# The last matrix of an expert layer multiplied over picked experts only, on one Trainium2 core

## The chip, the core and the metric

The kernel runs on one core of a Trainium2 chip, in one launch. The metric is the device time of that launch in microseconds (us). TensorE's matmuls are called PE, its weight loads PEld, VectorE DVE, ScalarE ACT, GpSimd POOL; SP is the queue that issues most of the loads.

## What is computed

Two transformer blocks on 256 tokens of width 2048, in float32. The second one ends in a layer of 16384 experts, 128 x 128 pairs of keys: each token picks 16 experts in each of 8 heads, and only the picked ones count for it.

```python
def block(xt):                                   # 128 tokens at a time
    q = (xt @ wq).reshape(-1, PEER_HEADS, 2, PEER_HALF)
    s = jnp.einsum('thpc,hpnc->thpn', q, keys)
    sv, si = lax.top_k(s, PEER_TOPK)
    ...
    top_s, top_j = lax.top_k(cand, PEER_TOPK)
    eid = jnp.take_along_axis(cid, top_j, axis=-1)
    gate = jax.nn.softmax(top_s.astype(jnp.float32), axis=-1)
    ue = jnp.take(u, eid, axis=0)
    act = jax.nn.gelu(jnp.einsum('thkd,td->thk', ue, xt).astype(jnp.float32), approximate=False)
    ve = jnp.take(v, eid, axis=0)
    return jnp.einsum('thk,thkd->td', (gate * act).astype(xt.dtype), ve)
...
h = layernorm(ALPHA * h + ff, ln2_g[l], ln2_b[l])
```

## The kernel before

All weights come as chunks of 128 x 1024 in the order of their use, through `Stream`: SP loads a chunk into `raw`, ACT copies it to `whi` (its upper bits, line 116), DVE subtracts to get `wlo` (line 99), some chunks ahead of PE. A product of float32 matrices is three matmuls of such parts: `colmm` (lines 265 to 267) with the weights standing, `tokmm` (lines 272 to 274) with the tokens standing. `Fill` holds side work as generators; `tick()` between chunks lets each go one step further, so the written order of the ticks sets where the side work stands in each engine's queue. No scheduler moves anything.

The last two stages take all experts, dense. In the u stage a tile `i1` is one first key with its 128 second keys, two chunks, 48 matmuls of 256 columns; there are 128 tiles and two ticks in each. The gelu of a tile goes into the activations, tiles of 128 experts x 256 tokens held in three buffers, `fx` (0 to 31), `act0` (32 to 55) and `act1` (56 to 127). From tile N0 = 56 on the side work is `weigh`: by groups of four tokens it makes one-hot vectors of each token's 128 pairs of keys (`eq` and `o2` by DVE, line 1195, two tokens an instruction; three products on POOL with the gates, lines 1198 and 1200), multiplies them on PE (line 1223, eight small matmuls a group) and so gets the sums of the gates of all pairs of keys. Tiles that are there are multiplied by them on DVE (line 1214), for the others they are copied into the place by ACT (line 1216) and the tile's gelu is multiplied later (line 1246). A group takes two ticks.

In the v stage the columns are done in two halves, 128 chunks each: `split` makes two parts of a tile's activations (ACT line 1260, DVE line 1261), and each chunk is multiplied with both halves of the tokens into four accumulators, 12 matmuls of 512 columns. The residual and the last norm's rows are loaded by POOL in between (lines 1292 and 1294). At the end come the last norm's statistics (`evac3`, `stats3`) and `apply3` by blocks of 512 columns on DVE (lines 1327, 1328) or ACT and POOL (lines 1323 to 1325), and the stores.

Of the kernel before, what the change touches and what calls it, by code (L numbers as in the profile page):

```python
# [13 lines left out]
U32 = mybir.dt.uint32  # L14
AF = mybir.ActivationFunctionType
# [5 lines left out]
D = 2048  # L21
KT = 16
T = 256
# [12 lines left out]
AHEAD = 3  # L36
GSCALE = 1024.0

# column table: per-feature parameters, one column of 128 features each
# [3 lines left out]
# row table: parameters broadcast over the partitions  # L43
# [3 lines left out]
class Stream:  # L47
    """Weight chunks [128, 1024] in the order of their use: loaded ahead, and split into two
    parts of 12 significant bits each that add up to the value. The first `n0` chunks have
    buffers of their own, those in `whole` stay as they are, and those in `extra` are split into  # L50
    the slots of `slots`, so that more of them than usual can be held."""
# [14 lines left out]
    def part(self, c, x):  # L66
        """a buffer for the first or the second part of chunk c, if there is one"""
# [76 lines left out]
class Fill:  # L144
    """Work that runs between the chunks of the products, on two lanes."""
# [35 lines left out]
def block(ctx, tc, a):  # L181
# [4 lines left out]
    # the weight chunks in the order of their use  # L186
# [40 lines left out]
    ch += [a["v"][i] for i in range(256)]  # L227
# [17 lines left out]
    # those of no use to the last stage  # L245
# [16 lines left out]
    def colmm(ps, w, wl, xh, xl, first, last, own=True):  # L262
        """ps += w' x in three products of parts"""
# [5 lines left out]
    def tokmm(ps, xh, xl, w, wl, first, last, own=True):  # L269
        """ps += x' w in three products of parts"""  # L270
# [5 lines left out]
    # ------------------------------------------------------------------ modulation  # L276
# [36 lines left out]
    # silu(c), silu(c_ctx) in two parts  # L313
# [19 lines left out]
    def stats_x(l):  # L333
# [14 lines left out]
        # var ** -1/2, and a Newton step  # L348
# [84 lines left out]
    def rope_gen(tile_):  # L433
        """axial rope in place on tile_[:, 0:2, :T]"""
# [98 lines left out]
    def gate_evac(ps, half, g):  # L533
        """mixed = silu(gate) * attention, in two parts"""
# [19 lines left out]
    def in_block(kind, half, g, ps):  # L554
        """a block of 256 columns, chunk by chunk"""
# [85 lines left out]
    # lam  # L641
# [27 lines left out]
    # ------------------------------------------------------------------ first output, norms  # L669
# [101 lines left out]
    def apply(tt):  # L771
        """the normed tokens in place, with the mean in mv and the scale in sm[3]"""
# [9 lines left out]
    def stats1(tt):  # L782
        # the first norm's scale r and the second's are one: r (r^2 var + e)^-1/2 = (var + e / r^2)^-1/2
# [399 lines left out]
    def weigh(l):  # L1183
# [6 lines left out]
        def onehots(n):  # L1190
            if n >= T // 2:
                return
# [251 lines left out]
```

## Time and profile before

| | |
|---|---|
| median of 3 runs | 2898.07 us (2896.87 to 2898.65) |
| span of the profiled execution | 2896.3 us |
| PE busy in the span | 2836.4 us, 18864 matmuls |
| DVE, ACT, POOL busy | 1920.3, 1270.1, 489.3 us |
| moved by DMA | 522.44 MB |

The profile is of one execution. The u stage runs from 1382 us (its first loads) to 2179 us, the v stage from there to the end. Matmuls are pipelined, so the duration of a single one is longer than the time from one to the next; the latter is what counts.

### The profile page before, as it was taken

The numbers are of one execution on the slowest core, as the hardware profiler recorded it, in microseconds if no ns is written. First come the engines' busy times: TensorE is split into PE (matmuls) and PEld (weight loads), VectorE is DVE, ScalarE is ACT, GpSimd is POOL, SyncE is SP. The second block draws the span as 40 slices with busy tenths as digits, with TensorE's granted clock in tenths as the row PEclk, the third lists the DMA queues.
The fourth block names the chain that finished last, engine by engine and source line by source line (L and its number), as shares of the span: only waits on it lengthen the run. The fifth ranks groups of instructions, "written<-read, shape, count | busy, mean of one in ns | idle before, by whom it ended". The sixth has DMA issues, their size and how long they took to land.

```text
span 2896.3 us, 47924 instructions
## 1 busy us (share of the span) xinstructions
PE 2836.4 (98%) x18864; PEld 2536.3 (88%) x18864; DVE 1920.3 (66%) x3028; ACT 1270.1 (44%) x1865; POOL 489.3 (17%) x564
## 2 busy tenths in 40 slices
PE   6999999999989999999999999999999999999997
PEld 1588889889879999989999999999998888888885
DVE  7766556444566665564888879999965656666566
ACT  6533334224454444454444444444445545455453
POOL 2000010000120000001000018888830000000001
PEclk8999999999999999999999999999999999999998
DMA  9734345444645555656666555555557666676664
GB/s 335 282 114 132 126 125 186 148 133 130 215 155 186 175 161 176 196 181 197 204 182 182 183 176 167 162 167 163 165 174 220 194 191 196 197 218 195 191 195 138
DMA packets 143650, 522.44 MB, mean 180 GB/s; under 512 B 16496, under 2 KB 16768, under 8 KB 143168
## 3 DMA queue, kind: packets, MB, share of 16 engines
q1 hardware_dynamic: 133648, 484.40, 53.4%
q0 software_dynamic: 9344, 34.32, 3.7%
q8 instruction: 148, 2.42, 0.3%
q14 instruction: 78, 0.64, 0.1%
q10 hardware_dynamic: 432, 0.66, 0.1%
HBM read 515.12 MB, written 4.19 MB: 179 GB/s over the span
## 4 chain that ended last, share of the span: by engine, by line
PE 92%; DVE 3%; DMA 2%; ACT 1%; issue 1%; POOL 0%; SPq 0%; DVEq 0%; ACTq 0%; POOLq 0%
PE acc L265 16%; PE acc L267 16%; PE acc L266 16%; PE acc L273 8%; PE acc L272 8%; PE acc L274 8%; PE lane L273 4%; PE lane L274 4%; PE lane L272 4%; PE acc L372 2%; PE lane L1223 1%; DMA raw<-in_w_out 1%; DVE wlo L99 1%; PE lane L452 1%; PE lane L478 0%
## 5 line engine op out<-in xcount | busy, mean ns | idle before, releaser
L99 DVE TENSOR_TENSOR wlo<-raw,whi 128x1024 fp32r<-128x1024 f32 x881 | 1116.1, 1270 | 620.1 <-issue 167.0
L116 ACT CAST whi<-raw 128x1024 fp32r<-128x1024 f32 x881 | 922.8, 1050 | 1074.5 <-PE acc L266 399.7
L265 PE MATMUL acc<-ga,whi 128*128 128x256 f32 x3024 | 862.3, 285 | 0.0
L267 PE MATMUL acc<-ga,wlo 128*128 128x256 f32 x3024 | 855.4, 283 | 0.4 <-DVE wlo L99 0.4
L266 PE MATMUL acc<-gb,whi 128*128 128x256 f32 x3024 | 855.4, 283 | 0.0
L267 PEld LDWEIGHTS acc<-ga,wlo 128*128 128x128 f32 x3024 | 578.9, 191 | 0.6 <-DVE wlo L99 0.6
L266 PEld LDWEIGHTS acc<-gb,whi 128*128 128x128 f32 x3024 | 579.3, 192 | 0.0
L265 PEld LDWEIGHTS acc<-ga,whi 128*128 128x128 f32 x3024 | 579.2, 192 | 0.0
L1198 POOL TENSOR_TENSOR o<-small,tab 128x256 f16<-128x256 f16 x256 | 282.9, 1124 | 142.5 <-DVE small L1195 116.5
L274 PE MATMUL acc<-whi,gb 128*128 128x512 f32 (+1 forms) x640 | 235.4, 368 | 0.0
L265 PE MATMUL acc<-Xh,whi 128*128 128x256 f32 (+1 forms) x704 | 230.4, 327 | 0.0
L267 PE MATMUL acc<-Xh,wlo 128*128 128x256 f32 (+1 forms) x704 | 224.5, 319 | 0.0
L266 PE MATMUL acc<-Xl,whi 128*128 128x256 f32 (+1 forms) x704 | 223.7, 318 | 0.0
L272 PE MATMUL acc<-whi,gb 128*128 128x512 f32 x512 | 199.3, 389 | 0.8 <-ACT gb L1260 0.8
L273 PE MATMUL acc<-wlo,gb 128*128 128x512 f32 x512 | 199.2, 389 | 0.0
L272 PE MATMUL lane<-whi,gb 128*128 128x512 f32 x512 | 199.2, 389 | 0.0
L273 PE MATMUL lane<-wlo,gb 128*128 128x512 f32 x512 | 199.2, 389 | 0.0
L274 PE MATMUL lane<-whi,gb 128*128 128x512 f32 x512 | 199.2, 389 | 0.0
L265 PEld LDWEIGHTS acc<-Xh,whi 128*128 128x128 f32 x704 | 132.7, 188 | 18.1 <-issue 5.7
L1261 DVE SCALAR_TENSOR_TENSOR gb<-act,gb 128x256 fp32r<-128x256 f32 x192 | 81.6, 425 | 97.8 <-ACT gb L1260 97.7
L266 PEld LDWEIGHTS acc<-Xl,whi 128*128 128x128 f32 x704 | 132.6, 188 | 12.5 <-issue 2.6
L267 PEld LDWEIGHTS acc<-Xh,wlo 128*128 128x128 f32 x704 | 132.2, 188 | 9.9
(357 smaller groups left out, 3995.1 us busy)
## 6 DMA issues: line engine op xcount, KB each, us to landing
raw<-in_u SPq DMA_DIRECT2D x256, 512.0 KB, 3.6
raw<-in_v SPq DMA_DIRECT2D x256, 512.0 KB, 4.3
raw<-in_w_in SPq DMA_DIRECT2D x240, 512.0 KB, 3.6
raw<-in_w_mod SPq DMA_DIRECT2D x64, 512.0 KB, 6.9
raw<-in_w_out SPq DMA_DIRECT2D x64, 512.0 KB, 4.3
gw<-in_w_mod POOLq DMA_DIRECT2D x32, 512.0 KB, 4.1
raw<-in_wq SPq DMA_DIRECT2D x32, 512.0 KB, 4.0
bc<-in_rows POOLq DMA_DIRECT2D x20, 256.0 KB, 8.1
```

The costliest lines, as they stand in the source:

```text
L99: e.tensor_tensor(lo, raw, hi.bitcast(F32), op=OP.subtract)
L116: nc.scalar.copy(hi, self.raw[c])
L265: mm(ps, w, xh, start=first and own, stop=False, **kw)
L266: mm(ps, w, xl, start=False, stop=False, **kw)
L267: mm(ps, wl, xh, start=False, stop=last, **kw)
L272: mm(ps, xh, w, start=first and own, stop=False, **kw)
L273: mm(ps, xh, wl, start=False, stop=False, **kw)
L274: mm(ps, xl, w, start=False, stop=last, **kw)
L372: mm(ps[0:4], c[:, k, :], w[:, j, :], start=k == 0 and w is parts[0], stop=k == KT - 1 and w is parts[-1])
L452: mm(s, qT[i * 64:i * 64 + 64, m, ts], kT[i * 64:i * 64 + 64, m, :], start=True, stop=True)
L1198: pool.tensor_tensor(o1s[n % 3][:, j], eq, tab[:, 2 + j, ts, None].to_broadcast([128, 2, 128]), op=OP.mult)
L1261: dve.scalar_tensor_tensor(wl, act_tile(n % 128), 1 / GSCALE, wh.bitcast(F32), op0=OP.mult, op1=OP.subtract)
```

## The change

The last stage multiplies only experts that some token picked, in blocks of 128 picked ones, whose rows of v and of the activations are gathered from memory by lists that the kernel makes itself.

*In the u stage.* One-hots are made on DVE alone, one token and one table at a time, six instructions for two tokens (POOL's products are gone). A third matmul for each token adds up, for each half of the tokens, the weights of each expert (`cnt`): where the sum is above 0, the expert is picked. There is a third tick in each tile from 56 on, and `weigh` ends before tile N1 = 100. `lists` then numbers the picked experts of the first 124 tiles (NKEY) by running sums on DVE and two small matmuls: those picked by both halves (and any that overflow) get places in up to 124 blocks M, those of the left or right half alone 29 blocks each (CL), L and R. POOL scatters the experts' numbers to their places in a list in DRAM, 124 indirect DMAs of 128 words, reads the list back and makes two index tables. From tile 99 on SP stores all activations of tiles 0 to 123 to DRAM (`rows`), 31 stores.

*In the v stage.* An item is a block of 128 experts with all 2048 columns. First the 4 last tiles whole (D, by plain loads), then alternately M with L and M with R, at last 5 M and 12 R: 4 + 51 (CM) + 29 + 29 items. POOL gathers an item's rows of v (128 x 8 KB) six items ahead and its activations (128 x 1 KB) three ahead, ACT and DVE split both two ahead. D and M are multiplied with both halves of the tokens, 24 matmuls, L and R with one, 12 matmuls. After the last L the count of M's places is compared on all engines, and if it is above 51 x 128 the other 73 blocks are done one after another (`rest`). The left half's norm and stores run beside the last 12 items, whose last three are multiplied bank by bank. v is laid out as rows of 2048 instead of two halves.

The diff, cut to its core:

```diff
+N1 = 100
+NKEY, CL, CM = 124, 29, 51
+TAIL, HELD, PFV = 12, 3, 6
...
-ch += [a["v"][i] for i in range(256)]
...
     def weigh(l):
+        cnt = lane(1 - l)
         def onehots(n):
...
-            for x, j in ((eq, 0), (o2s[n % 3], 1)):
-                dve.tensor_tensor(x, iota[:, None, :].to_broadcast([128, 2, 128]),
-                                  tab[:, j, ts, None].to_broadcast([128, 2, 128]), op=OP.is_equal)
-            for j in range(2):
-                pool.tensor_tensor(o1s[n % 3][:, j], eq, tab[:, 2 + j, ts, None].to_broadcast([128, 2, 128]),
-                                   op=OP.mult)
-            pool.tensor_tensor(o2s[n % 3], o2s[n % 3], scale[:, ts, None].to_broadcast([128, 2, 128]), op=OP.mult)
+            for i in range(2):
+                t = 2 * n + i
+                for j in range(2):
+                    dve.tensor_scalar(o1[:, i, j], iota, tab[:, 0, t:t + 1], tab[:, 1 + j, t:t + 1],
+                                      op0=OP.is_equal, op1=OP.mult)
+                dve.tensor_scalar(o2[:, i], iota2, tab2[:, 0, t:t + 1], tab2[:, 1, t:t + 1],
+                                  op0=OP.is_equal, op1=OP.mult)
...
+                    for j in range(2):
+                        mm(q[:, i * 128:i * 128 + 128], o2, o1[:, j], start=j == 0, stop=j == 1)
+                    t = 4 * g + i
+                    h = t // 128 * 128
+                    mm(cnt[:, h:h + 128], o2, o1[:, 0], start=t % 128 == 0, stop=t % 128 == 127)
...
+        yield from lists(l, cnt)
+    def lists(l, cnt):
...
+        for tt in range(2):
+            dve.tensor_scalar(m[tt], cnt[:, tt * 128:tt * 128 + NKEY], 0.0, None, op0=OP.is_gt)
...
+        for i in range(NKEY):
+            d = pool.indirect_dma_start(
+                out=lst, out_offset=bass.IndirectOffsetOnAxis(ap=at[:, i:i + 1], axis=0), in_=e[:, i:i + 1],
+                in_offset=None, bounds_check=128 * WL - 1, oob_is_err=False)
...
+        pool.dma_start(el, lst2)
...
+        pool.tensor_copy(lact, el)
+        pool.tensor_scalar(lv, el, 1.0, -1.0, op0=OP.max, op1=OP.add)
...
+    def keep(i, n):
+        x, j = act_at(i)
+        out = rows[1 + i * 128:1 + (i + n) * 128, :].rearrange("(n p) t -> p n t", p=128)
+        nc.sync.dma_start(out, x[:, j:j + n, :])
...
+                if j == 3 and half and i1 >= N0:
+                    fill.tick()
...
+        if N1 <= i1 + 1:
+            for _ in range(2 if (i1 - N1) % 4 else 1):
+                if order:
+                    keep(*order.pop(0))
+            if i1 >= N1 + 4 and (i1 - N1) % 4 == 0:
+                keep(i1 - 4, 4)
...
+    def split_v(raw, hi, lo):
+        for h in range(2):
+            x = raw[:, h * 1024:h * 1024 + 1024]
+            act.copy(hi[h], x)
+            dve.tensor_tensor(lo[h], x, hi[h].bitcast(F32), op=OP.subtract)
...
+    for n in range(PFV):
+        fetch_v(n)
+    for n in range(2):
+        split(n)
...
+    for n in range(len(items)):
+        if n + PFV < len(items):
+            fetch_v(n + PFV)
+        if n + 3 < len(items):
+            fetch_a(n + 3)
+        if n + 2 < len(items):
+            split(n + 2)
...
+        if n < len(items) - HELD:
+            for b in range(4):
+                item(n, b)
+        if n == over:
+            many = nc.values_load(number, min_val=0, max_val=NKEY * 128)
+            with tc.If(many > CM * 128):
+                rest()
+        if n == lastof[0]:
+            fill.add_side(first_half())
+        elif n > lastof[0]:
+            fill.tick(2)
```

DVE's queue for one group of `weigh`, before: a split chunk (`wlo`), the three products of the group before (L1214), two one-hots for two tokens at a time (L1195), the product with a tile's gelu (L1246).

```order
L99 TENSOR_TENSOR wlo<-raw,whi 128x1024
L1195 TENSOR_TENSOR small<-iota,tab 128x256
L1195 TENSOR_TENSOR o_17286<-iota,tab 128x256
L99 TENSOR_TENSOR wlo<-raw,whi 128x1024
L1214 TENSOR_TENSOR fx<-fx,lane_18459 128x32x4
L1214 TENSOR_TENSOR act_13325<-act_13325,lane_18459 128x24x4
L1214 TENSOR_TENSOR act_17252<-act_17252,lane_18459 128x14x4
L1195 TENSOR_TENSOR small<-iota,tab 128x256
L1195 TENSOR_TENSOR o_17284<-iota,tab 128x256
L1246 TENSOR_TENSOR act_17252<-act_17252,acc 128x52
```

The same place now; twelve one-hots (L1215, L1217) stand together between the splits (L107) and the products (L1243, L1369).

```order
L107 TENSOR_TENSOR wlo<-raw,whi 128x1024
L1243 TENSOR_TENSOR fx<-fx,lane_17592 128x32x4
L1243 TENSOR_TENSOR act_13334<-act_13334,lane_17592 128x24x4
L1243 TENSOR_TENSOR act_17266<-act_17266,lane_17592 128x3x4
L1215 TENSOR_SCALAR o_17750<-iota,tab 128x128 x2
L1217 TENSOR_SCALAR o_17749<-iota_13321,tab_13320 128x128
L1215 TENSOR_SCALAR o_17750<-iota,tab 128x128 x2
L1217 TENSOR_SCALAR o_17749<-iota_13321,tab_13320 128x128
L1215 TENSOR_SCALAR o_17758<-iota,tab 128x128 x2
L1217 TENSOR_SCALAR o_17757<-iota_13321,tab_13320 128x128
L1215 TENSOR_SCALAR o_17758<-iota,tab 128x128 x2
L1217 TENSOR_SCALAR o_17757<-iota_13321,tab_13320 128x128
```

Three products on POOL and two wide instructions on DVE have become six narrow ones on DVE for two tokens.

POOL's queue from the end of `weigh` to the end of the kernel, before: the last products, the plain loads for the last norm, and then the norm's own work (L257 is the inverse root, L1324 and L1325 the products of `apply3`).

```order
L1198 TENSOR_TENSOR o_17289<-small,tab 128x256 x2
L1200 TENSOR_TENSOR o_17286<-o_17286,scale 128x256
L1294 DMA ga<-spill 128x512 x8
L1292 DMA fx<-in_rows 128x512 x8
L257 TENSOR_TENSOR small<-small,nhalf 128x1
L1324 TENSOR_TENSOR ga<-ga,fx 128x512
L1325 TENSOR_TENSOR ga<-ga,fx 128x512
```

POOL's queue now, at the same place: the scatters (L1310), the list read back, and the gathers of v (`in_v`) and of the activations (`rows`), which go on through the whole stage.

```order
L1307 IOTA tab 128x124
L1310 DMA lst<-tab,o_22197 23296x1 x124
L1319 DMA o_23067<-lst 128x182
L1322 CAST tab<-o_23067 128x182
L1323 TENSOR_SCALAR tab_23070<-o_23067 128x182
L1420 DMA act_24462<-in_v,tab_23070 128x2048 x2
L1420 DMA fx<-in_v,tab_23070 128x2048 x2
L1420 DMA act_24462<-rows,tab 128x256
L1420 DMA fx<-in_v,tab_23070 128x2048
L1420 DMA act_24462<-rows,tab 128x256
```

And POOL's queue in the last items: the inverse root (L264) and the products of the left half's norm (L1505, L1506) stand ahead of the last activations' gathers.

```order
L264 TENSOR_TENSOR small<-small,nhalf 128x1
L1420 DMA act_24462<-in_v,tab_23070 128x2048
L1420 DMA act_24462<-rows,tab 128x256
L1505 TENSOR_TENSOR ga<-ga,gb 128x512
L1506 TENSOR_TENSOR ga<-ga,gb 128x512
L1505 TENSOR_TENSOR ga<-ga,gb 128x512
L1506 TENSOR_TENSOR ga<-ga,gb 128x512
L1420 DMA act_24462<-rows,tab 128x256
L1505 TENSOR_TENSOR ga<-ga,gb 128x512
L1506 TENSOR_TENSOR ga<-ga,gb 128x512
L1505 TENSOR_TENSOR ga<-ga,gb 128x512
L1506 TENSOR_TENSOR ga<-ga,gb 128x512
L1420 DMA act_24462<-rows,tab 128x256 x2
```

All indirect transfers have come onto POOL, 124 + 218 of them, and the plain loads of the residual and of the norm's rows have moved from POOL to SP.

## Rows read from the trace of the kernel before

**Rows 1.** The page: PE's part of the span, clock by slices, chain by engine.

```profile
PE 2836.4 (98%) x18864; PEld 2536.3 (88%) x18864; DVE 1920.3 (66%) x3028; ACT 1270.1 (44%) x1865; POOL 489.3 (17%) x564
PEclk8999999999999999999999999999999999999998
PE 92%; DVE 3%; DMA 2%; ACT 1%; issue 1%; POOL 0%; SPq 0%; DVEq 0%; ACTq 0%; POOLq 0%
```

**Rows 2.** Stretches: length, busy by engine (instructions), PEclk, DMA share, GB/s.

```profile
1900.00:2138.00 238.00, 238.00 (x2076) 230.51 (x2075) 217.47 (x370) 102.76 (x186) 201.88 (x218) 1.00 0.54 165
2179.00:2530.00 351.00, 350.22 (x1546) 289.82 (x1545) 212.27 (x262) 177.34 (x262) 4.91 (x9) 1.00 0.66 200
2530.00:2868.00 338.00, 338.00 (x1493) 279.85 (x1492) 208.72 (x257) 169.40 (x248) 3.83 (x7) 1.00 0.65 198
```

**Rows 3.** Instructions of a line: durations in ns (min/median/max), first and last start.

```profile
L1248 ACT ACTIVATE fx<-acc x32: 383/384/386, 1403.2 to 1582.2; 128x256 f32<-128x256 f32 x32
L1245 ACT ACTIVATE acc<-acc x71: 158/275/368, 1734.0 to 2179.2; 128x256 f32<-128x256 f32 x8, 128x4 f32<-128x4 f32 x1, 128x8 f32<-128x8 f32 x1, 128x12 f32<-128x12 f32 x1
L1246 DVE TENSOR_TENSOR act<-act,acc x71: 146/292/422, 1734.6 to 2179.6; 128x256 f32<-128x256 f32 x8, 128x4 f32<-128x4 f32 x1, 128x8 f32<-128x8 f32 x1, 128x12 f32<-128x12 f32 x1
```

**Rows 4.** Chain in order of time: start, us, what; one such for each group.

```profile
1740.37 0.62 PE lane L1223 x8
```

**Rows 5.** Waits from 1700 us on: who waited for whom, us, times, longest.

```profile
PE acc L272 <- ACT gb L1260: 0.8, 1, 0.8
PEld L1223 <- POOL o L1200: 11.1, 64, 1.0
```

**Rows 6.** DVE in order of time: start, us, instruction.

```profile
835.19 1.36 DVE L810 TENSOR_SCALAR zf<-lane,cols 128x128 f32<-128x128 f32 x4
940.82 1.11 DVE L919 TENSOR_SCALAR hm<-hm,mq 128x128 f32<-128x128 f32 x4
1720.96 1.23 DVE L99 TENSOR_TENSOR wlo<-raw,whi 128x1024 fp32r<-128x1024 f32 x1 [1.65 <-PE acc L267]
1722.10 0.42 DVE L1195 TENSOR_TENSOR small<-iota,tab 128x256 f16<-128x256 f16 x1
...
2002.91 0.27 DVE L1214 TENSOR_TENSOR fx<-fx,lane 128x128 f32<-128x128 f32 x1
2003.11 0.48 DVE L1214 TENSOR_TENSOR act<-act,lane 128x96 f32<-128x96 f32 x2
2003.52 0.80 DVE L1195 TENSOR_TENSOR small<-iota,tab 128x256 f16<-128x256 f16 x1
```

**Rows 7.** POOL's plain DMAs by line: issue in ns, us from issue to landing.

```profile
L1294 POOL DMA_DIRECT2D ga<-spill x8: 546/546/599, 2179.4 to 2183.3; - x8
L680 POOL DMA_DIRECT2D res<-in_x x4: 712/712/734, 750.4 to 754.2; - x4
L682 POOL DMA_DIRECT2D bc<-in_rows x4: 564/564/567, 751.1 to 754.9; - x4
...
DMA to landing us min/median/max: 7.0/12.0/14.8
```

**Rows 8.** DMA issues of POOL: count, size, median us to landing.

```profile
gw<-in_w_mod POOLq DMA_DIRECT2D x32, 512.0 KB, 4.1
spill<-res POOLq DMA_DIRECT2D x1, 2048.0 KB, 9.3
```

**Rows 9.** Two early stretches, for the transfer rate: columns as in rows 2.

```profile
10.00:15.00 5.00, 3.35 (x12) 0.78 (x10) 2.45 (x2) 3.61 (x5) 0.00 (x0) 1.00 1.03 420
40.00:60.00 20.00, 18.89 (x75) 6.01 (x75) 17.61 (x26) 10.98 (x15) 0.00 (x0) 1.00 0.85 300
```

**Rows 10.** Groups by form from 1500 us on: busy us, mean ns, idle before.

```profile
L116 ACT CAST whi<-raw 128x1024 fp32r<-128x1024 f32 x473 | 496.8, 1050 | 490.6 <-DMA raw<-in_v 153.7 <-PE acc L266 136.3 <-PE acc L274 107.1
L1260 ACT ACTIVATE gb<-act 128x256 fp32r<-128x256 f32 x192 | 78.7, 410 | 0.0
```

**Rows 11.** The end in order of time: start, us, instruction.

```profile
2876.23 1.49 POOL L1324 TENSOR_TENSOR ga<-ga,fx 128x512 f32<-128x512 f32 x1 [1.12 <-ACT ga L1323]
2877.80 1.59 POOL L1325 TENSOR_TENSOR ga<-ga,fx 128x512 f32<-128x512 f32 x1
2878.19 0.67 DVE L1265 SCALAR_TENSOR_TENSOR ga<-ga,lane 128x512 f32<-128x512 f32 x1
```

More of the change, by code (lines that the diff above doesn't have):

```diff
@@ L1217, in weigh @@
                 done["tokens"] = 4 * g
+                yield
             if g < T // 4:
[L1219 to L1226 removed]
+                p = q
+        yield from lists(l, cnt)
@@ new lines, in block, with act_at, act_tile @@
+    number = pg.tile([1, 1], I32, name="number")
+    places = []
+    def keep(i, n):
+        x, j = act_at(i)
+        out = rows[1 + i * 128:1 + (i + n) * 128, :].rearrange("(n p) t -> p n t", p=128)
+        nc.sync.dma_start(out, x[:, j:j + n, :])
+    def act_at(i1):
+        for i, j, x in acts:
+            if i1 < j:
+                return x, i1 - i
+    def act_tile(i1):
+        x, j = act_at(i1)
+        return x[:, j, :]
+    order = [(i, 4) for a0, b0 in ((N0, N1), (0, 32), (32, N0)) for i in range(a0, b0, 4)]
@@ L1241, in block @@
                 colmm(ps[:, :T], hi[:, j, :], lo[:, j, :], h1h[:, k], h1l[:, k], k == 0, k == KT - 1)
+                if j == 3 and half and i1 >= N0:
+                    fill.tick()
             fill.tick()
+        if i1 == N1 - 1:
+            while done["tokens"] < T:
+                fill.tick()
         n, x = done["tokens"], act_tile(i1)
@@ L1249, in block @@
         done["tiles"] = i1 + 1
-    fill.drain()
+        if N1 <= i1 + 1:
[4 more added lines that the diff above has]
+                keep(i1 - 4, 4)
+    fill.drain()
+    lact, lv = places
+    items = [("D", i) for i in range(NKEY, 128)]
+    m, left, right = ([(x, b + i) for i in range(n)] for x, b, n in
+                      (("M", 0, CM), ("L", NKEY, CL), ("R", NKEY + CL, CL)))
@@ new lines, in block @@
+    for a0, n in ((left, len(left)), (right, len(right) - TAIL)):
+        for i in range(n):
+            items += [m.pop(0), a0.pop(0)]
+    items += m + right
+    over = items.index(("L", NKEY + CL - 1))
+    halves = {"D": (0, 1), "M": (0, 1), "L": (0,), "R": (1,)}
+    fx = tp.tile([128, 4, D], F32, name="fx")
+    x0 = ap0.tile([128, 3, D], F32, name="act0")
+    x1 = ap1.tile([128, (N1 - N0) * T], F32R, name="act1")
+    raws = [fx[:, i] for i in range(4)] + [x0[:, i] for i in range(2)]
@@ new lines, in block, with pair, fresh @@
+    acs = [x0[:, 2, i * T:i * T + T] for i in range(8)]
+    part = x1[:, 8192:].rearrange("p (n t) -> p n t", t=T)
+    def pair(x, i):
+        return [x[:, i * D + h * 1024:i * D + h * 1024 + 1024] for h in range(2)]
+    def fresh(name):
+        return [sp.tile([128, 1024], F32R, name=n, bufs=BUFS[("raw", "whi", "wlo").index(n)]) for n in name]
+    his = [pair(x1, i) for i in range(2)] + [fresh(["whi", "whi"])]
+    los = [pair(x1, 2 + i) for i in range(2)] + [fresh(["wlo", "wlo"])]
+    banks = [[lane(0), lane(0), lane(1), lane(1)], [acc() for _ in range(4)]]
@@ new lines, in block, with fetch_v, gather @@
+    opened = set()
+    def fetch_v(n):
+        kind, i = items[n]
+        if kind == "D":
+            nc.sync.dma_start(raws[n % len(raws)], a["v"][i * 128:i * 128 + 128, :])
+        else:
+            gather(raws[n % len(raws)], a["v"], lv, i)
+    def gather(out, src, places, i):
+        pool.indirect_dma_start(
+            out=out, out_offset=None, in_=src,
+            in_offset=bass.IndirectOffsetOnAxis(ap=places[:, i:i + 1], axis=0),
+            bounds_check=src.shape[0] - 1, oob_is_err=False)
@@ new lines, in parts_of, with split, products @@
+    def parts_of(n):
+        return part[:, n % 5], part[:, 5 + n % 5]
+    def split(n):
+        kind, i = items[n]
+        split_v(raws[n % len(raws)], his[n % len(his)], los[n % len(los)])
+        x = act_tile(i) if kind == "D" else acs[n % 7]
+        ts = slice(halves[kind][0] * 128, halves[kind][-1] * 128 + 128)
+        split_a(x[:, ts], *(y[:, ts] for y in parts_of(n)))
+    def products(tt, b, hi, lo, wh, wl, last):
+        ts, bs = slice(tt * 128, tt * 128 + 128), slice(b % 2 * 512, b % 2 * 512 + 512)
+        tokmm(banks[tt][b], wh[:, ts], wl[:, ts], hi[b // 2][:, bs], lo[b // 2][:, bs], not (tt, b) in opened, last)
+        opened.add((tt, b))
@@ new lines, in block, with item, rest @@
+    lastof = [max(n for n, x in enumerate(items) if tt in halves[x[0]]) for tt in range(2)]
+    def item(n, b):
+        for tt in halves[items[n][0]]:
+            products(tt, b, his[n % len(his)], los[n % len(los)], *parts_of(n), n == lastof[tt])
+    for n in range(PFV):
+        fetch_v(n)
+    for n in range(2):
+        split(n)
+    def rest():
+        raw = ap1.tile([128, D], F32, name="late")
+        hi, lo = fresh(["whi", "whi"]), fresh(["wlo", "raw"])
+        for i in range(CM, NKEY):
+            gather(raw, a["v"], lv, i)
+            gather(acs[7], rows, lact, i)
+            split_v(raw, hi, lo)
+            split_a(acs[7], part[:, 10], part[:, 11])
+            for b in range(4):
+                for tt in range(2):
+                    products(tt, b, hi, lo, part[:, 10], part[:, 11], False)
```

226 lines of the change are left out of this document (135 added, 91 removed).

## The prediction

> **What bounds the kernel now.** The page comes first. PE is busy for 98% of the span and is 92% of the chain that ended last, at full granted clock nearly throughout [rows 1]. The windows by stage say the same of the two stages that the change touches: in the u stage (to 2179 us) and in the v stage (2179 to 2878 us) PE has no idle time worth naming, while the DMA engines are some two thirds busy [rows 2]. So time is gained or lost here by the number of matmuls, until another engine falls behind PE. The prices of PE's work: a matmul of 512 columns in the v stage costs 338.00 / 1493 = 0.2264 us [rows 2]; a u tile without one-hot work costs (1582.2 - 1403.2) / 31 = 5.774 us, and with it (2179.2 - 1734.0) / 70 = 6.36 us [rows 3]; one group of four tokens adds 0.62 us for 8 small matmuls (64 such rows), 0.0775 us each [rows 4].
>
> **What the picking is worth.** Before, each of 128 blocks of experts is multiplied with both halves of the tokens: 256 half-blocks of 12 matmuls. Now there are 4 whole blocks (D), 51 for both halves (M), 29 for the left half (L) and 29 for the right (R): 8 + 102 + 58 = 168. That the lists fit is not in the trace; I counted it by working the reference's own top-k on its inputs: of the first 124 blocks' experts 6216 are picked by both halves (51 blocks hold 6528), 3694 and 3649 by one alone (29 hold 3712), so the guarded rest of 73 blocks should not run. Removed: 88 x 12 x 0.2264 = **-239.1 us**, all on the chain.
>
> **The count in the u stage.** One more 128-column matmul for each token, 256 x 0.0775 = **+19.8 us** on PE. A u tile now has three ticks instead of two, so a group of four tokens takes two thirds of a tile: 2/3 x 5.774 + 12 x 0.0775 = 4.78 us of PE time.
>
> **One-hots on VectorE.** POOL's three products for two tokens vanish; PE's weight loads waited 11.1 us for them over 64 groups, beside matmuls that went on [rows 5], so that gives nothing. VectorE had two instructions for two tokens and gets six, of half the width. In a group's 4.78 us it also splits 4/3 chunks, 1.14 us each from start to start, does three products of a group, 0.61 us [rows 6], and two thirds of a product with the gelu, 0.19 us [rows 3]: 2.32 us. For the twelve one-hots no row has 16-bit data. The nearest is the 128x128 form with two pointer scalars: four in 1.11 us, the last 0.34 long, so 0.256 us apart; from PSUM four in 1.36, so 0.32 apart [rows 6]. I take 0.24, a little under the nearest row since the elements are half as wide. 12 x 0.24 + 2.32 = 5.2 us: VectorE becomes the bound of this stretch by 0.4 us a group, 64 x 0.4 = **+26 us**. The bounds are 0 and, at 0.32, 64 x 1.38 = +88. The row has 0.256 us for 128 columns of 4 bytes [rows 6]. The Trainium skill ("VectorE: DVE Perf Modes", section on the TRN2 errata) says that an SBUF operation pays a fixed cost each time, so many small tiles pay it often, which speaks against this change; but by its figures, 58 cycles and 128/4 columns at 0.96 GHz, one instruction is estimated at 94 ns, and the stretch would stay PE's and the sum 26 us less.
>
> **Listing and scattering.** The lists' few VectorE and PE steps lie between chunks, with up to two split chunks in hand: **+3 us** (0 to 10). Then POOL issues 124 scatters of 128 words, each after the landing of the eighth one before it. Their cover: the last group is done at tick 128, in tile 98; the scatter can start some five ticks later, at tile 100.3. Up to the first gathered item PE still has 27.7 x 5.774 = 160 us of u, about 4 us of start and 4 D blocks of 24 x 0.2264 = 5.43 us, 186 us in all. About 20 us of it go to the last landing, reading the list back, two small POOL operations, five gather issues, a landing and a split, at 0.55 us an issue and 4.1 us a landing [rows 7, 8]. So a scatter may cost 166 / 124 = 1.34 us before PE waits. The trace has no indirect DMA. From below, POOL needs 0.546 us to issue a plain DMA of 128 rows and 0.712 for 256 [rows 7]; from above, the longest landing seen, 14.8 us, shared by eight gives 1.85 [rows 7]. I take 1.1, twice the plain issue, for an address looked up for each row: **hidden, 0 us**. At 1.85 it costs 124 x 1.85 - 166 = +63.
>
> **Writing the rows.** 31 stores of 512 KB go on SP's queue, two a tile from tile 99 on: 2.1 MB each 5.774 us with the u loads behind them, 363 GB/s. The DMA engines gave 420 GB/s over 5 us and 300 over 20 [rows 9]. I take **+4 us**; at 300 GB/s for 13 tiles it is +16, at 420 nothing.
>
> **Start of the v stage.** Before, chunks of v were split ahead of the last gelu and PE waited 0.8 us [rows 5]. Now both copies of 1.05 us [rows 10] and the activations' split come behind the last gelu on ScalarE, VectorE's two splits behind them: **+3 us**.
>
> **Inside the v stage.** An M and an L or R together are 36 x 0.2264 = 8.15 us on PE. ScalarE needs 4 x 1.05 + 0.7, VectorE 4 x 1.14 + 0.65 = 5.2 [rows 6, 10], POOL four issues of 1.1, and the DMA engines 2.36 MB, 5.6 us at 420 GB/s. All are hidden. The last 12 items are R alone, 2.72 us each: 1.18 MB needs 2.8 us, with six blocks fetched ahead, so no loss by transfers. The guard for the rest is a meeting point: each engine waits for all the others and for each DMA in flight, loads the count and branches. The trace shows nothing like it; between nothing (the queues stand full two items ahead) and two landings of 4.1 us [rows 8] with a drained PE, about 12, I take **+5 us**.
>
> **The end.** The first half's norm now runs in the last 12 items, and POOL holds it: four blocks with two products of some 1.5 us each [rows 11], and the activations' gathers of the last three items queue behind them (order rows above). PE is through the others 9 x 2.72 = 24.5 us after the last M. The rsq comes some 14 us after it, ScalarE's first apply at 16, POOL's eight products end at 29, the last gathers are issued, landed and split by about 35, while the held items need them at 25: **+9 us** (0 to 14). From the last matmul to the end the steps are much as before (18 us from 2878.2 [rows 11]), with fewer applies left: **-1 us**.
>
> **Sum.** -239.1 + 19.8 + 26 + 3 + 0 + 4 + 3 + 5 + 9 - 1 = -170 us against the profiled span of 2896.3 us, so 2726. The median of the runs lies 1.8 us over that span (2898.07): **2728 us**.
>
> **Rivals.** *Late scatter.* POOL's scatter takes 1.85 us each and PE stands at the first M item: 2728 + 63 = 2791. For it: 14.8 us landings occur when transfers pile up [rows 7], and here stores and loads share the engines; against it: the usual 4.1 us, by eight, is 0.5. The Trainium skill ("DMA: Bandwidth & Descriptors", "Anatomy of one DMA") gives each small POOL-issued DMA a fixed 2.0 us, estimated 124 x 2.0 = 248 us if nothing overlapped; it also says that most of this is waiting for completion, which eight in flight share; no run yet shows which. *Slow gathers.* If rows arrive as the 2 MB spill did, in 9.3 us [rows 8], 225 GB/s, a pair takes 10.5 us instead of 8.15: 46 x 2.35 = +108, 2835. Against it, plain loads ran at 420. *Cheap one-hots.* At 0.2 us apart or less the group needs 12 x 0.2 + 2.32 = 4.72 us of VectorE, under PE's 4.78, and the +26 goes: 2702. Against it, no row of this form stands under 0.25 us [rows 6]; for it, none has 16-bit data. *POOL as the bound, slower than before.* At x us an indirect issue, scatter and stage together cost (124x - 166) + (218x - 445), where 445 us is PE's time for the 164 gathered half-blocks. This eats the 170 us from x = 2.28 on; at 2.5 us, 2728 + 144 + 100 = 2972. For it: one POOL instruction with 128 looked-up addresses can be several times the plain one; against it, 256 rows cost only 0.17 us more than 128. *The change doesn't leave out what it says*: if the guarded rest ran, 73 blocks with nothing fetched ahead, some 12 us each (a landing, a split, 5.43 of PE), it would be +880 us; only a miscount could do it.
>
> **Chances.** Forecast 0.60 (its own range 2690 to 2790, from the bounds of the one-hots, the guard, the stores and the end); late scatter 0.14; slow gathers 0.11; cheap one-hots 0.08; POOL as the bound 0.06; the rest running 0.01. The range that leaves out no more than 2 in 10 is 2680 to 2835. A measurement here can tell about 0.2%, 6 us, from no change. Faster 0.93; within it 0.01, a POOL price near 2.28; slower 0.06.
>
> **What would show it.** Right: 12 x 168 matmuls of 0.226 us in the last stage; u tiles 56 to 98 at some 7.8 us with PE waiting for VectorE's one-hots or splits; POOL's scatter over before PE starts the first M; a gap of a few us in the middle of the v stage on all engines; PE waiting for the activations' split in the last items. Wrong: a long PE gap after the D blocks (late scatter); PE waiting for v rows all through (slow gathers, or POOL busy all along); one-hots under 0.2 us apart.

## The result, and the profile after

The changed kernel takes **2769.97 us** (median of four runs, 2764.47 to 2771.09) against 2898.36 us for the kernel before on the same chip: a ratio of 0.9552, 95% interval 0.9539 to 0.9566. That is 128 us less. The forecast was 2728 us, 42 us too low; the measured time lies inside its range of 2680 to 2835. The profiled execution is the fastest of the four, 2764.47 us with a span of 2762.7, so in its own terms the change is worth 2896.3 - 2762.7 = 133.6 us.

The page of the changed kernel, to be read beside [rows 1]: PE, DVE and POOL in 40 slices of 69 us each, and TensorE's granted clock.

```profile
PE 2623.1 (95%) x18070; PEld 2358.7 (85%) x18070; DVE 1803.4 (65%) x3396; ACT 1184.6 (43%) x1741; POOL 576.0 (21%) x519
PE   6999999999999999999999999998989949999995
DVE  7666566443565765555488887999984426666656
POOL 2000000000012000001000000000017875666654
PEclk8999999999999999999999999999999979999997
```

PE's share fell from 98% to 95%: the kernel before had no slice like the "4" in PE's row (2210 to 2279 us). In it DVE is at 2, POOL at 7 or 8, and the granted clock falls to 0.7. This is where most of the missing gain is. The next rows show the place: PE in order of time (start, duration in us, instruction, in brackets the idle time ahead of it and what ended it), POOL at the end of the scatter, and ScalarE.

```profile
2245.70 0.39 PE L281 MATMUL acc<-act 128*128 128x512 f32 x1
2280.51 0.79 PE L279 MATMUL lane<-act 128*128 128x512 f32 x1 [34.41 <-ACT act L1437]
```

```profile
2258.67 0.97 POOL L1310 DMA_INDIRECT lst<-tab,o  x1 [0.30 <-issue]
2261.36 0.59 POOL L1319 DMA_DIRECT2D o<-lst  x1 [1.72 <-issue]
2263.68 0.34 POOL L1322 CAST tab<-o 128x182 uint32<-128x182 f32 x1 [1.73 <-DMA o<-lst]
2264.00 0.88 POOL L1323 TENSOR_SCALAR tab<-o 128x182 uint32<-128x182 f32 x1
2265.15 1.17 POOL L1420 DMA_INDIRECT act<-in_v,tab  x1 [0.28 <-POOL tab L1323]
...
2270.53 1.01 POOL L1420 DMA_INDIRECT act<-rows,tab  x1 [0.30 <-issue]
```

```profile
2271.38 1.99 ACT L1433 CAST act<-act 128x1024 fp32r<-128x1024 f32 x2 [40.39 <-DMA act<-in_v,tab]
2280.04 0.42 ACT L1437 ACTIVATE act<-act 128x256 fp32r<-128x256 f32 x1 [6.66 <-DMA act<-rows,tab]
```

PE has done the last D block at 2246.1 us and stands for 34.4 us. The last scatter (L1310) is issued only at 2258.7. Behind it come the list's read-back, two small POOL operations, the gathers, the landing of the first rows and their split, 20.9 us to PE's restart. The prediction had 20 for this chain. So the chain is as foreseen, and it is the scatter that ends late. After the gap the granted clock is 0.56 (2281 to 2284 us), and PE's first matmuls are 0.42 to 0.59 us apart in place of 0.23, which costs another 1.6 us. The scatter's rows, and those of the one-hots and of the u stage (durations in ns, minimum, median, maximum, then first and last start):

```profile
L1310 POOL DMA_INDIRECT lst<-tab,o x124: 972/976/1983, 2063.9 to 2258.7; - x124
DMA to landing us min/median/max: 2.1/5.2/7.2
```

```profile
L1229 PE MATMUL lane<-o,o x512: 216/219/230, 1721.3 to 2043.3; 128*128 128x128 f16 x171
L1371 ACT ACTIVATE fx<-acc x32: 384/384/385, 1401.0 to 1579.9; 128x256 f32<-128x256 f32 x32
L1368 ACT ACTIVATE acc<-acc x72: 181/358/384, 1729.9 to 2219.1; 128x256 f32<-128x256 f32 x30, 128x4 f32<-128x4 f32 x1, 128x8 f32<-128x8 f32 x1, 128x16 f32<-128x16 f32 x1
```

The scatter: (2258.7 - 2063.9) / 123 = 1.58 us from start to start, where 1.1 had been taken. The cover that the trace gives is 2246.1 - 20.9 - 2063.9 = 161 us, or 1.30 us each (the prediction: 166 us, 1.34). The u stage ends 42.2 us later against its own 32nd tile than before ([rows 3]: 2179.2 - 1582.2 = 597.0; now 2219.1 - 1579.9 = 639.2).

The windows of the changed kernel (length, busy time of PE, PEld, DVE, ACT, POOL with instructions, granted clock, DMA share, GB/s): the stretch of the scatter under u, the steady v stage, and the end, from the statistics of the left half's first block to those of the right half's last.

```profile
2064.00:2219.00 155.00, 155.00 (x1293) 154.88 (x1291) 72.83 (x79) 61.51 (x77) 126.30 (x95) 1.00 0.90 295
2300.00:2500.00 200.00, 200.00 (x874) 163.54 (x873) 130.84 (x146) 113.94 (x146) 126.42 (x98) 1.00 0.75 285
2694.88:2747.23 52.35, 37.42 (x131) 26.44 (x129) 35.18 (x45) 21.86 (x30) 28.96 (x20) 0.84 0.34 118
```

PE is busy for all of the first stretch, although the DMA engines are at 0.90, so the stores cost PE nothing. It is busy for all of the second, so the gathers keep up: no trace of the rival of slow gathers. In the third it has 131 matmuls, at 200.00 / 874 = 0.2288 us each 30.0 us of work, and takes 52.35: 22.4 us are lost, of which 52.35 - 37.42 = 14.9 are idle. The other 7.5 are work that took longer, at a granted clock of 0.84.

### The profile page after: what moved, and what is told of

The parts are those of the page before. It is cut to its first block, busy times and chain, and to the rows that moved or that the text cites. A ratio compares the mean times of both kernels' runs of the same rounds, so it can differ in the third digit from the quotient of the medians.

```text
span 2762.7 us, 46040 instructions
## 1 busy us (share of the span) xinstructions
PE 2623.1 (95%) x18070; PEld 2358.7 (85%) x18070; DVE 1803.4 (65%) x3396; ACT 1184.6 (43%) x1741; POOL 576.0 (21%) x519
## 5 line engine op out<-in xcount | busy, mean ns | idle before, releaser
L107 DVE TENSOR_TENSOR wlo<-raw,whi 128x1024 fp32r<-128x1024 f32 x625 | 762.6, 1225 | 524.0 <-PE acc L274 167.5
L124 ACT CAST whi<-raw 128x1024 fp32r<-128x1024 f32 x625 | 651.3, 1049 | 710.0 <-PE acc L273 319.3
L1434 DVE TENSOR_TENSOR act<-fx,act 128x1024 fp32r<-128x1024 f32 x114 | 140.4, 1237 | 98.8 <-ACT act L1433 96.9
L1310 POOL DMA_INDIRECT lst<-tab,o x124 | 158.2, 1276 | 60.6 <-issue 37.5
L1433 ACT CAST act<-fx 128x1024 fp32r<-128x1024 f32 x114 | 118.9, 1048 | 112.4 <-PE acc L281 105.6
L279 PE MATMUL acc<-whi,Xh 128*128 128x256 f32 x480 | 136.4, 284 | 0.0
L1215 DVE TENSOR_SCALAR o<-iota,tab 128x128 f16<-128x128 f16 x512 | 136.3, 309 | 0.0
L1420 POOL DMA_INDIRECT act<-rows,tab x109 | 128.5, 1179 | 34.9 <-issue 33.2
L281 PE MATMUL acc<-whi,Xl 128*128 128x256 f32 x480 | 134.6, 280 | 0.0
L280 PE MATMUL acc<-wlo,Xh 128*128 128x256 f32 x480 | 134.6, 280 | 0.0
```

Of the source, the lines that this page charges most:

```text
L107: e.tensor_tensor(lo, raw, hi.bitcast(F32), op=OP.subtract)
L124: nc.scalar.copy(hi, self.raw[c])
L279: mm(ps, xh, w, start=first and own, stop=False, **kw)
L280: mm(ps, xh, wl, start=False, stop=False, **kw)
L281: mm(ps, xl, w, start=False, stop=last, **kw)
L1215: dve.tensor_scalar(o1[:, i, j], iota, tab[:, 0, t:t + 1], tab[:, 1 + j, t:t + 1], op0=OP.is_equal, op1=OP.mult)
```

## The experiments

Each run was measured on one chip beside the kernel before, which had 2898.0 to 2898.6 us each time, so times from different chips are compared below. Of the changed kernel's own time there are two measurements, 2769.97 and 2770.74 us; the first three runs, and the result stores on SP's queue, are set against the first.

**Is it the scatter's end? The scatter halved.**

```
-        for i in range(NKEY):
+        for i in range(0, NKEY, 2):
             d = pool.indirect_dma_start(out=lst, ...)
```

> Only every second column of the list is scattered, 62 instead of 124 (the other picked experts are left out: their places point to row 0); the gathers and products that follow keep their number. Theory A (gap from the late end of the scatter): 62 x 1.58 = 98 us, no gap, 2735 us. Theory B (gap from the start of the gathered blocks): 2765 to 2775.

2728.38 us (2725.94 to 2730.34; ratio 0.9418, 0.9402 to 0.9434): 42 us less, 35 expected. The gap after the D blocks is gone; the longest wait left for L279 at the start of the v stage is 2.8 us. The 62 scatters took from 2065.2 to 2168.2 us, 1.69 us each. Theory A holds: the gap is the late scatter, and nothing else of the start of the gathered blocks shows once it is early.

**The same scatter, begun sooner.** The top-k gets a third tick on odd tiles, and the count begins at tile 48:

```
-                if j == 3 and half and i1 >= N0:
+                if j == 3 and half and (i1 >= START or i1 % 2):
...
-        if i1 == N0:
+        if i1 == START:
```

> The counting and the listing start eight tiles of u sooner (tile 48 instead of 56): the top-k gets a third tick on every second tile before. The scatter keeps its price but begins 8 x 5.77 = 46 us sooner against the end of u. Theory A (PE's 35 us gap after the D blocks is the scatter ending late, 124 x 1.58 = 196 us against a cover of 161): the gap is gone, the time is 2770 - 35 = 2735 us. Theory B (the gap is the start of the gathered blocks itself: reading the list back, first gathers, splits, some 20 us with the queues full): the gap stays near 35 us and so does the time, 2765 to 2775.

2743.46 us (2741.60 to 2745.29; ratio 0.9466, 0.9451 to 0.9482): 27 us less, not 35. The scatter began at 2023.3 us but now took 1.71 us each, and a gap of 6.2 us stayed. Nearly all of it ran beside VectorE's splits; in the changed kernel the last 21 scatters ran beside an idle VectorE. Theory A again, with a price that seems to depend on what VectorE does.

**What makes a scatter last 1.6 us?** VectorE's splits beside the scatter are taken away:

```
+                if c >= n - 2 * (128 - N1):
+                    nc.scalar.copy(lo, raw)
+                else:
                     e.tensor_tensor(lo, raw, hi.bitcast(F32), op=OP.subtract)
```

> For the last 28 tiles of u the second part of each chunk is a plain copy by ScalarE in place of VectorE's subtraction, so the last 28 tiles' low parts are wrong and VectorE has hardly any work beside the scatter. Theory A (a scatter costs 1.28 us by itself and is drawn out by VectorE's two-input subtraction): 1.28 us each, 159 us in all, PE's gap nearly gone, 2733 to 2740 us. Theory B (drawn out by the DMA engines, which are full there with stores and loads): still 1.58 us each, 2770.

2731.45 us (2730.50 to 2732.20; ratio 0.9426, 0.9410 to 0.9442): 39 us less, a little more than expected. The scatter's row in this run, and the window beside it:

```profile
L1313 POOL DMA_INDIRECT lst<-tab,o x124: 972/974/1099, 2063.7 to 2221.2; - x124
```

```profile
2064.00:2220.00 156.00, 156.00 (x1303) 156.00 (x1302) 11.36 (x27) 111.28 (x132) 118.81 (x123) 1.00 0.91 295
```

(2221.2 - 2063.7) / 123 = 1.28 us each, with the DMA engines as full as in the changed kernel (0.91 against 0.90, 295 GB/s in both). So full DMA engines do not draw it out; VectorE does. The changed kernel's own rows show how, POOL first and then DVE:

```profile
2096.79 0.97 POOL L1310 DMA_INDIRECT lst<-tab,o  x1 [0.30 <-issue]
...
2099.51 1.57 POOL L1310 DMA_INDIRECT lst<-tab,o  x1 [0.31 <-issue]
...
2102.68 1.70 POOL L1310 DMA_INDIRECT lst<-tab,o  x1 [0.30 <-issue]
2104.68 0.97 POOL L1310 DMA_INDIRECT lst<-tab,o  x1 [0.30 <-issue]
```

```profile
2099.01 1.22 DVE L107 TENSOR_TENSOR wlo<-raw,whi 128x1024 fp32r<-128x1024 f32 x1
2102.30 1.22 DVE L107 TENSOR_TENSOR wlo<-raw,whi 128x1024 fp32r<-128x1024 f32 x1 [2.07 <-ACT whi L124]
2104.66 1.28 DVE L107 TENSOR_TENSOR wlo<-raw,whi 128x1024 fp32r<-128x1024 f32 x1
```

A scatter that begins while a split is running ends 0.85 us after the split does: 2099.51 + 1.57 = 2101.08 against 2099.01 + 1.22 = 2100.23, and 2104.38 against 2103.52. Of the 51 scatters that begin inside a split of the u stage, 50 end 0.83 to 0.94 us after it. The exception is the last one shown: it begins 0.02 us after its split's start and has its plain 0.97 us, and that split takes 1.28 us. The other way round there is hardly a wait: the 25 splits that begin inside a scatter take their usual 1.22 or 1.23 us. So the scatter waits for the split's end and does not share with it. The Trainium skill ("SBUF — State Buffer", section "Who interferes with whom") says that a VectorE instruction with two SBUF inputs contends with a GpSimd instruction that reads SBUF, and that the port pair which the two share is an exclusive lock. The trace agrees where the split comes first; it shows no split held for the 0.97 us of a scatter. The same section says, as an inference, that such an instruction does not hold up the making of DMA descriptors; for the issue of these indirect DMAs the 1.57 and 1.70 us beside 0.97 say otherwise. Whether the reading of the places or the making of the descriptors waits, no run shows.

**The stores moved away from the scatter.**

```
-        if N1 <= i1 + 1:
-            for _ in range(2 if (i1 - N1) % 4 else 1):
+        if 117 <= i1:
+            for _ in range(3):
...
-            if i1 >= N1 + 4 and (i1 - N1) % 4 == 0:
-                keep(i1 - 4, 4)
+            if i1 == 120:
+                for i in range(N1, 120, 4):
+                    order.append((i, 4))
```

> The 31 stores of the activations' rows start at tile 117 of u instead of 99, so no store stands beside the scatter until 2160 us. Theory A (VectorE's two-input subtraction draws the scatter out): each scatter costs as before, 1.6 to 1.7 us from start to start in the u stage. Theory B (stores and loads together fill the DMA engines and draw it out): 1.28 us in the stretch without stores. The time itself says little here, since the first gathers wait for the last stores, about 2770 to 2790 us.

One run, 2884.48 us. For most of the scatter it tells nothing on its question: on this chip PE nearly stood still, and so VectorE had hardly any splits beside it. But PE was still busy in the first 38 us, where no store had been issued yet:

```profile
2067.00:2105.00 38.00, 38.00 (x319) 38.00 (x318) 18.25 (x20) 15.65 (x20) 30.82 (x23) 1.00 0.57 179
```

In this window the 23 scatters start 1.70 us apart (2067.49 to 2104.93), although the DMA engines are at 0.57. In the changed kernel's first 38 us they start 1.56 us apart at a DMA share of 1.00. So Theory A holds here too. PE's standstill came also in the next three kernels, which ran beside this one. The windows of the run with the rows gathered six items ahead, in the scatter and after it, and PE in order of time:

```profile
2100.00:2230.00 130.00, 20.38 (x54) 15.41 (x54) 2.78 (x3) 2.36 (x3) 99.31 (x101) 0.50 0.07 18
2250.00:2290.00 40.00, 40.00 (x335) 40.00 (x335) 18.25 (x20) 16.33 (x21) 0.00 (x0) 1.00 1.04 368
```

```profile
2116.99 0.37 PE L273 MATMUL acc<-gb,whi 128*128 128x256 f32 x1 [2.44 <-issue]
2119.11 0.37 PE L274 MATMUL acc<-ga,wlo 128*128 128x256 f32 x1 [1.75 <-issue]
2121.91 0.37 PE L272 MATMUL acc<-ga,whi 128*128 128x256 f32 x1 [2.43 <-issue]
```

From about 2095 us to the scatter's end PE starts a matmul mostly every 0.7 to 2.8 us and waits for nothing that the profile shows ("issue"); 54 in 130 us, where some 1080 would fit (1293 in 155 us above). POOL's scatters go on at 1.28 us each, the loads have all but stopped (DMA share 0.07; SP's queue waits up to 65.4 us for a split), and the clock is granted at 0.50, its lower level. After the last scatter all is as usual. It is not the stores: with them moved away it was the same. The times of these four kernels lie 66 to 115 us above the changed kernel's. What follows from them is read from their traces, before and after that stretch.

**The one-hots: is VectorE the bound of the count's stretch?**

```
-                for j in range(2):
+                for j in range(1):
                     dve.tensor_scalar(o1[:, i, j], iota, tab[:, 0, t:t + 1], ...)
...
-                        mm(q[:, ...], o2, o1[:, j], start=j == 0, stop=j == 1)
+                        mm(q[:, ...], o2, o1[:, 0], start=j == 0, stop=j == 1)
```

> VectorE makes 8 one-hots for a group of four tokens instead of 12: the one that carries the gate's low part is left out, and the matmul that used it takes the high part's again, so PE's work is the same and the gates are wrong. Theory A (VectorE is the bound of the count's stretch, 12 x 0.224 + 2.32 = 5.01 us a group against PE's 4.78): 64 x (5.01 - 4.78) = 15 us less, about 2755 us, and the stretch's 64 groups at 4.78 us. Theory B (PE waits there for ScalarE's copies into the tiles, which follow PE): 2768 to 2771.

The time, 2836.42 us, holds PE's standstill. The stretch itself lies ahead of it, the count's first matmul of a token by its line, and the window:

```profile
L1229 PE MATMUL lane<-o,o x512: 216/219/230, 1724.9 to 2011.5; 128*128 128x128 f16 x171
```

```profile
1725.00:2011.00 286.00, 285.66 (x2750) 282.89 (x2748) 254.02 (x815) 125.62 (x289) 0.24 (x1) 1.00 0.47 153
```

286.6 us for 64 groups, 4.48 each, with PE busy throughout, against 322.0 us and 5.03 in the changed kernel. Theory A holds, and is worth 35.4 us in this stretch, not 15: PE's own share of a group is 4.48, not 4.78.

**The end: which queue holds it?** Three edits. The left half's result stores moved from ScalarE's queue to SP's (`e = nc.scalar if by_pool and tt else nc.sync`); the rows gathered six items ahead (`fetch_a(n + 6)`); and both.

> The first half's four result stores go out on SP's queue instead of ScalarE's; nothing else changes. Theory A (at the end ScalarE waits in its own queue for POOL's norm products, 13 us in four waits, with the copies of the last gathered blocks behind it, and PE idles for those): most of PE's 14 us of idle time there goes, 2758 to 2764 us. Theory B (as predicted: POOL's products stand ahead of the last gathers in POOL's queue): nothing moves, 2770.

> The activations' rows are gathered six items ahead instead of three, so all of them stand ahead of the first half's norm products in POOL's queue. Theory A (the prediction's: the last gathers queue behind POOL's eight norm products, and with the stores on SP's queue ScalarE indeed waited for late rows instead): most of PE's idle 14 us at the end goes, 2770 - 9 = 2761 us, 2757 to 2764. Theory B (ScalarE's queue, where the result stores wait for POOL's products, holds it): 2766 to 2771.

> As the run with the rows gathered six ahead, and the first half's four stores on SP's queue as well. Theory A: little more than that run, within 3 us of it. If the two queues hold it in turn, each hidden behind the other: 5 us or more below that run, about 2755 us. The shared port of POOL and VectorE would leave VectorE's splits of 1.2 us at up to 2.6 us beside POOL's products in both.

The stores alone: 2772.15 us (2763.37 to 2774.93), no gain. The other two times, 2863.29 and 2864.09 us, hold PE's standstill, so the end is read from the traces. The end's window in the three kernels, in this order, as for the changed kernel above (52.35 us there):

```profile
2701.87:2753.91 52.04, 37.93 (x131) 27.44 (x129) 38.78 (x44) 21.72 (x30) 29.92 (x20) 0.80 0.35 119
```

```profile
2807.64:2859.48 51.84, 39.57 (x131) 27.77 (x129) 35.01 (x45) 21.91 (x30) 23.85 (x17) 0.77 0.31 112
```

```profile
2791.89:2838.51 46.62, 35.74 (x131) 25.85 (x129) 40.85 (x44) 21.48 (x30) 28.09 (x17) 0.85 0.35 124
```

Either edit alone gives 0.3 to 0.5 us, both together 5.7, each read from one execution. The two queues hold the end in turn. The changed kernel's ScalarE shows the one, and with the stores gone from its queue ScalarE shows the other:

```profile
2717.13 0.81 ACT L1504 ACTIVATE ga<-ga,small 128x512 f32<-128x512 f32 x1 [5.26 <-POOL ga L1506]
2726.60 0.81 ACT L1504 ACTIVATE ga<-ga,small 128x512 f32<-128x512 f32 x1 [3.86 <-POOL ga L1506]
```

```profile
2725.26 0.31 ACT L1437 ACTIVATE act<-act 128x128 fp32r<-128x128 f32 x1 [4.19 <-DMA act<-rows,tab]
2740.47 0.31 ACT L1437 ACTIVATE act<-act 128x128 fp32r<-128x128 f32 x1 [7.92 <-DMA act<-rows,tab]
```

In the first two rows ScalarE waits for POOL's products, with the copies of the last blocks behind; in the last two it waits for rows whose gathers stand behind the same products on POOL. With both edits VectorE was busy 40.85 us in place of 35.18, POOL's products now running beside its splits; that this is what still cost time there is not shown.

**The changed kernel once more, and two versions.** All of the next four ran beside each other. The second begins the count at tile 46, holds POOL's norm products back until the last split is issued (eight more `yield`s ahead of them), and has the left half's stores on SP's queue. The third makes one of the three one-hots on POOL: `(pool if j else dve).tensor_scalar(o1[:, i, j], ...)`. The fourth has all of it.

> The changed kernel with no edit, beside the next three. In four runs on one chip PE stood nearly still during the scatter, with an instruction only every 1.4 us and nothing awaited, and their times were 60 to 115 us longer; on another chip no run showed it. If it belongs to the chip and not to those four edits, this kernel has 2764 to 2773 us where its scatter runs beside a busy PE, and about 2870 us where PE stands still.

> Counting and listing from tile 46 of u (57.7 us sooner), the first half's norm products on POOL only after the last item's split is issued, and its stores on SP's queue. Theory (the scatter's late end costs 35 us and a slow clock after it; the end costs 14 us of PE's idle time because POOL's products and ScalarE's stores hold the last gathers and copies): no gap after the D blocks, -40 us, and -8 us at the end, so 2722 us, or 48 us under the unchanged kernel of this call. Rival (VectorE has no room for three steps of the top-k on every second tile): the u stage grows by 10 us or more and half of the gain goes.

> The one-hot with the gate's low part is made on POOL, which is idle in that stretch; VectorE makes 8 for a group instead of 12. Theory A (VectorE is the bound of that stretch; with 8 one-hots the run without the low parts had 4.48 us a group against 5.03): 64 x 0.55 = 35 us under the unchanged kernel. Theory B (POOL's instruction takes over 1.1 us, four a group, or draws out VectorE's two-input instructions through the shared port): less than 10 us, or slower.

> The edits of the two runs before together. If they are independent, their gains add up: 48 + 35 = 83 us under the unchanged kernel, some 2687 us. If POOL is too slow for the one-hots, its loss shows here as there.

The unchanged kernel: 2770.74 us (2769.43 to 2773.06), with PE's gap of 35.7 us and no standstill. A standstill of some 130 us was seen on one chip of the three that these runs came from, in all four kernels there, and in none of the eight others.

The second: 2725.70 us (2721.97 to 2730.65; ratio to before 0.9399, 0.9383 to 0.9415), 45 us under the unchanged kernel, 48 expected. The third: 2736.85 us (2734.34 to 2738.64; 0.9442, 0.9426 to 0.9458), 34 us under it, 35 expected. The fourth: **2692.19 us** (2687.94 to 2693.43; 0.9283, 0.9267 to 0.9298), 78.5 us under it, the sum of the two gains being 78.9, and faster than both the kernel before and the changed one. First the end's window of the second, then the one-hots of the third:

```profile
2672.19:2711.87 39.68, 33.13 (x131) 24.83 (x129) 32.29 (x44) 21.40 (x30) 24.61 (x18) 0.96 0.41 142
```

```profile
L1215 POOL TENSOR_SCALAR o<-iota,tab x256: 786/894/1982, 1636.4 to 2011.8; 128x128 f16<-128x128 f16 x128
L1215 DVE TENSOR_SCALAR o<-iota,tab x256: 297/307/445, 1724.4 to 2011.4; 128x128 f16<-128x128 f16 x128
```

The end shrank from 52.35 to 39.68 us for the same 131 matmuls. POOL needs 0.89 us for a one-hot, four a group, 3.6 us of the group's 4.5: hidden.

## Why the prediction was right, and by how much it was not

By its steps, each against the profiled execution:

- **Products: -239.1 predicted, -234 measured.** 2016 matmuls at 0.2288 us are 461.3, where [rows 2] give 3072 x 0.2264 = 695.5. The guarded rest did not run.
- **Count and one-hots: +45.8 predicted, +38.8 measured, in other shares.** That the sum came near is luck: the count was put 16 us too high and the one-hots 9 too low. The stretch takes 322.0 us for 64 groups, and without them 42.7 tiles of 5.774 us would take 246.4: 75.6 us. Before, the 64 groups took 406.3 us (first matmul at 1726.5, last at 2132.8) over 64 tiles of 5.774, 369.5 us: 36.8 us. The difference is 38.8. The count was mis-sized: with 8 one-hots, where PE is the bound, all twelve matmuls of a group cost (286.6 - 246.4) / 64 = 0.63 us, as much as [rows 4] had for eight. That row's 0.62 us holds the run-out of its last matmul once, which lasts 0.22 us by itself, so an eighth of it is too much for one: a matmul costs 0.63 / 12 = 0.052 us, not 0.0775. At that price the 512 of before are 26.8 of their 36.8 us. The other 10 fit the 11.1 us that PE's weight loads waited for POOL's products [rows 5], which the prediction had put at nothing. So the count cost 13.4 us less these 10, a net +3.4. The one-hots came out 0.224 us apart, not 0.24, but cost 35.4 us, not 26, since PE's share beside them is 4.48 us. VectorE as the bound of this stretch was right: 12 x 0.224 + 2.32 = 5.01 us a group, 5.03 measured.
- **Lists and stores: +3 and +4 predicted, +3.4 together.** It is what remains of the 42.2 us; PE did not wait for transfers at 0.90 DMA share.
- **Scatter: 0 predicted, +34.4 measured. This is the step that failed**, and it is as large as the whole error of 36 us in the profiled execution: the other errors, up to 16 us each, cancel to some 2, which is luck. The prediction's own sign of being wrong here, a long PE gap after the D blocks, appeared; the time stayed inside the range because that was drawn to hold a late scatter too. The break-even was right (1.34 predicted, 1.30 by the trace), as was the chain of 20 us behind it. The price of 1.1 us, "twice the plain issue", was a guess that lay on the favourable side of a break-even only a fifth above it. POOL alone needs 0.97 and 0.30 us, 1.28 in all, just under the break-even; VectorE's splits add 0.3 us on the mean. The rival *late scatter* had the right place and the right shape (a long gap after the D blocks), with 1.85 us for 1.58 and with another cause: landings, at 2.1 to 7.2 us by eight in flight, never held it.
- **Start of v: +3 predicted, +2.4 measured.** PE lost 3.2 us around the last gelu, 0.8 before [rows 5].
- **Guard: +5 predicted, +2.0 measured**, 0.81 us for the branch and 1.19 a little later. The queues stood full, as the lower bound had it.
- **The end: +9 predicted, +22.4 measured.** The mechanism named, POOL's products ahead of the last gathers, is real but was only half: the same products also held ScalarE, through the result stores in its queue, which the prediction did not look at. And it counted idle time only; the granted clock of 0.84 in this stretch cost 7.5 us on top.
- **Tail: -1 predicted, -3.5 measured.** The last matmul ends 16.2 us before the end of the span (at 2746.5), and ended 19.8 us before it in the kernel before (at 2876.5). The prediction's 18 us counts from VectorE's reading of the last sums, at 2878.2 [rows 11].

-234 + 38.8 + 3.4 + 34.4 + 2.4 + 2.0 + 22.4 - 3.5 = -134.1 us, against -133.6 in the profiled execution.

Of the rivals, cheap one-hots (under 0.2 us), slow gathers and POOL as the bound of the whole did not happen: one-hots stood at 0.224 us, PE was busy 200.00 of 200 us in the v stage, and a gather's issue took POOL 1.0 to 2.05 us there, 1.3 on the mean. The sum of the rival on POOL counts 164 gathered half-blocks; there are 102 + 58 = 160, 435 us in place of 445, which moves its break-even only from 2.28 to 2.25 us.

What stays open is PE's standstill: it came with the scatter and ended with it, on one chip and not on two others, and it came also with the stores moved away and with fewer one-hots. The runs don't tell what held PE's instructions back. On such a chip most of the gain is lost (2863.29 us against 2898.63 with the rows gathered six ahead, ratio 0.9852, 0.9810 to 0.9894); the unchanged kernel was not run on it.

## What to carry to other kernels

When a term is put at nothing because it is covered, the ratio of price to break-even is the forecast: 1.1 against 1.34 us, with no row for the price, deserved a charge and a larger chance for the rival, not zero. On POOL price a DMA together with what VectorE does beside it, and look for work of two inputs on VectorE as for a queue; starting the covered work earlier, or giving VectorE's small operations to an idle POOL, gave most of the loss back here. At a kernel's end, list for every queue what stands behind the slow engine's result, the stores too: two queues can hold it in turn, and an edit of either one alone then shows nothing.

## What was not expected of the hardware

- An indirect DMA of 128 single words keeps POOL for 0.97 us and 0.30 us more to the next, and up to 1.98 us when it meets a VectorE instruction with two inputs; the plain DMA of [rows 7] took 0.55.
- The contention can go the other way: two of VectorE's splits, 2.34 us in a row alone, took up to 5.17 us beside POOL's norm products (run with the stores on SP's queue).
- A 128x128 one-hot costs VectorE 0.224 us from start to start (0.31 by its own duration) and POOL 0.89.
- A stream of small scatters went with a PE that starts a matmul only every 0.7 to 2.8 us, on one chip of three.
